# Query, key, value and forget-logit projection by one level of Strassen's algorithm

## The chip, the cores and the metric

The kernel runs on one NeuronCore of a Trainium2 chip: TensorE (PE in the profile; its weight loads are shown apart as PEld), VectorE (DVE), ScalarE (ACT), GpSimd (POOL) and SyncE (SP, which here only issues DMAs). The metric is the device time of one execution in microseconds; the profiled execution is a single run of its own.

## The reference, cut to what matters

One layer of an encoder over 2048 tokens of width 1024: a mixing block (attention with forget gates in eight heads of 64, beside a multi-scale pooling branch), cross-attention to 256 memory tokens, and a gated feed-forward part. All in float32. The change touches only the first projection and what is made of it:

```python
xn = rmsnorm(h, g_mix[l])
z = jnp.einsum('bsd,dc->bsc', xn, w_in[l])      # 1024 -> 2056 columns
q = z[..., :512]; k = z[..., 512:1024]; v = z[..., 1024:1536]
p_in = z[..., 1536:2048]                        # pooling branch
f_logit = z[..., 2048:] + b_forget[l]           # 8 columns
q = rmsnorm(head_split(q, 8, 64), g_q_fox[l])
k = rmsnorm(head_split(k, 8, 64), g_k_fox[l])
```

Queries, keys, values and forget logits are 1544 of the columns; the 512 of the pooling branch are projected by other code.

## The kernel before

Products are made to nearly float32 accuracy: `split` cuts an operand into a rounded part `hi` (ScalarE copies it to type fp32r) and the rest `lo` (VectorE subtracts, `sub_hi`, line 55, or with a gain `split_gain`, lines 173 and 174), and `mm3` (lines 60 to 62) issues three matmuls, hi·hi, hi·lo and lo·hi, into one PSUM bank.

The stages in order: (1) the keys and values of the memory tokens (`kv`, 96 matmuls 512 wide), while the weights `w_qkvf` (1024 by 1544) are loaded and split; (2) the projection studied here; (3) the pooling branch, in eight blocks of 256 tokens; (4) attention, cross-attention and feed-forward, which the change doesn't touch.

In stage 2 the weights lie split in SBUF, eight slices of 128 rows by 1544 columns. A loop runs over eight blocks `b` of 256 tokens and two tiles `i` of 128 tokens in each. For a tile, `project` makes four PSUM banks of 386 columns, each over eight slices of the 1024 rows: 4·8·3 = 96 matmuls. The transposed input `xT` is loaded once, in tiles of 128 by 2 by 256 (`x_load`), and split (`x_split`), which also makes the squares for the token norm; `token_sums` adds them up over partitions by matmuls against ones (line 199), two tiles at a time, and `token_rstd` makes the reciprocal root on GpSimd. ScalarE moves the banks to SBUF times that factor (`scaled`, line 324). `normed_heads` splits the values and makes the head norms, `split_heads` scales queries and keys by norm and by gain (lines 355, 357) and splits them, and `to_heads` turns them by four groups of four TensorE transposes (line 369, into a PSUM tile that ScalarE copies, line 371) and stores them to DRAM (`qkT`). Values go to `vd`.

In this stage all five engines run in the written order (`tc.manual_schedule`): what is written ahead of an instruction on its engine also goes ahead on the chip. The stage ends with the pooling projection of block 0 (`project_p`); behind it only TensorE's order is fixed, and the other engines' is made by the framework's scheduler.

The lines that carry the stage:

```python
for k, n in ([(k, n) for k in range(KD) for n in ns] if k_outer else [(k, n) for n in ns for k in range(KD)]):
    sl = slice(n * ZB, (n + 1) * ZB)
    mm3(zps[n][:], (hs[k][:, ts], ls[k][:, ts]), (whi[k][:, sl], wlo[k][:, sl]), k == 0, k == KD - 1)
```

Of the kernel before, what the change touches and what calls it, by code (L numbers as in the profile page):

```python
# [33 lines left out]
QKVF = 3 * FOXW + H  # L34
ZB = QKVF // 4

# [4 lines left out]
def block_kernel(ctx: ExitStack, tc: tile.TileContext, x, xT, memT, cols, rows, w_qkvf, w_p, w_pool, w_out,  # L41
# [52 lines left out]
    gqs = cst.tile([P, 2, DH], F32, name="gqs")  # L94

    dve.tensor_scalar(out=gqs[:, 0, :], in0=gqf, scalar1=-(DH ** -0.5), scalar2=None, op0=ALU.mult)
    dve.tensor_copy(gqs[:, 1, :], gkf)
    gqm = cst.tile([P, 1], F32, name="gqm")
    dve.tensor_scalar(out=gqm[:], in0=gq_mem, scalar1=P ** -0.5, scalar2=None, op0=ALU.mult)
    rstd = cst.tile([P, NT], F32, name="rstd")  # L100
# [24 lines left out]
    class Slots:  # L125

        def __init__(self, pl, shape, name, n):
            self.pl, self.shape, self.name = pl, shape, name
            self.free = list(range(n))

        def take(self, dt):
            n = self.free.pop(0)
            return n, self.pl.tile(self.shape, dt, tag=f"{self.name}{n}", name=f"{self.name}{n}", bufs=1)

    xsl = Slots(xp, [P, 2, B], "xl", 9)
    xlow = []

    def x_load(b, src=xTk, qs=range(4)):

        while len(xlow) > 4:  # L140
            xsl.free.append(xlow.pop(0))
        tiles = []
        for q in qs:
            n, raw = xsl.take(F32)
            sp.dma_start(raw[:], src[:, 2 * q:2 * q + 2, b * B:(b + 1) * B])
            tiles.append((n, raw))
        return tiles

    def x_split(tiles, part=None, qs=range(4)):

        for q in qs:
            n, raw = tiles[q]
            hi = xp.tile([P, 2, B], F32R, tag="xhi", name="xhi", bufs=8)
            act.copy(hi[:], raw[:])
            if part is not None:
                sq = xp.tile([P, 2, B], F32, tag="xsq", name="xsq", bufs=2)[:] if q else part
                act.activation(sq, raw[:], AF.Square, scale=1.0 / 32.0)
                if q:
                    pool.tensor_tensor(out=part, in0=part, in1=sq, op=ALU.add)
            m, lo = xsl.take(F32R)  # L160
            sub_hi(lo[:], raw[:], hi[:])
            xsl.free.append(n)
            xlow.append(m)
            tiles[q] = hi, lo
# [18 lines left out]
    whi = [None] * KD  # L183
    wlo = [None] * KD
    wph = [None] * KD
    wpl = [None] * KD
    HIS = 16

    with ExitStack() as c0:
        was = ExitStack()  # L190
        wa = opened(was, "wa", side="right")
        tpp = opened(xstack, "tpp", space=PSUM)

        def token_sums(part):

            ssp = tpp.tile([P, 2], F32, tag="ss", name="ss", bufs=1)
            for j in range(2):
                for c in range(2):
                    pe.matmul(ssp[:, j:j + 1], lhsT=part[:, c, j * P:(j + 1) * P], rhs=ones[:, 0:1], start=c == 0,
                              stop=c == 1)  # L200
            return ssp

        def token_rstd(ssp, outp):
            ms = xp.tile([P, 2], F32, tag="ms", name="ms", bufs=2)
            dve.tensor_copy(ms[:], ssp[:])
            rsqrt(outp, ms[:])


        kvs = ExitStack()
        kvp = opened(kvs, "kvp", space=PSUM)  # L210
        first = in_order(EN.DVE, EN.Activation, EN.Pool, EN.SP)
        first.__enter__()
        kv = [[kvp.tile([P, MW], F32, name=f"kv{m}{a}") for a in range(2)] for m in range(2)]
        wk = [None] * KD
        wsl = Slots(wa, [P, QKVF], "wl", KD)
        w_raw = [None] * KD

        def w_in_hi(k, dt):

            return wa.tile([P, QKVF], dt, tag=f"wh{k}", name=f"wh{k}", bufs=1)  # L220

        def load_kv(k):
            wk[k] = w_in_hi(k, F32)[:, :2 * MW]
# [8 lines left out]
        def load_w_in(k):  # L232

            n, raw = wsl.take(F32) if k < KD - 1 else (None, slab(3))
            w_raw[k] = n, raw[:, :QKVF]
            sp.dma_start(w_raw[k][1], w_qkvf[k * P:(k + 1) * P, :])

        def split_w_in(k):
            n, raw = w_raw[k]
            whi[k] = w_in_hi(k, F32R)  # L240
            wlo[k] = wsl.take(F32R)[1]
            split(whi[k][:], wlo[k][:], raw, g_mix[:, k:k + 1])
            wsl.free.append(n)
# [5 lines left out]
        xt = x_load(0)  # L249
        mpart = xp.tile([P, 2, B], F32, tag="part", name="part", bufs=1)  # L250
        mr = cst.tile([P, 2], F32, name="mr")
        for k in range(KD):
# [4 lines left out]
            if k == 3:  # L257
                token_rstd(token_sums(mpart), mr[:])
            for m in range(2):
                ms_ = slice(m * P, (m + 1) * P)  # L260
                for a in range(2):
                    as_ = slice(a * MW, (a + 1) * MW)
                    mm3(kv[m][a][:], (mh[:, ms_], ml[:, ms_]), (wh[:, as_], wl[:, as_]), k == 0, k == KD - 1)
            if k < 4:
                load_kv(k + 4)
            if k == 1:
                load_w_in(0)
            if k == 3:
                for c in range(1, KD):
                    load_w_in(c)  # L270
            if k == 6:
                split_w_in(0)
            if k == 5:
                part = xp.tile([P, 2, B], F32, tag="part", name="part", bufs=1)
                x_split(xt, part[:])
        split_w_in(1)
        mks_ = [slab(n, dt=F32R)[:].rearrange("p (a c) -> p a c", a=2) for n in (2, 0)]
        mkv = [t_[:, a] for t_ in mks_ for a in range(2)]
        mkh, mkl = (t_.rearrange("p (h m) -> p h m", h=MH) for t_ in mkv[:2])
        mvh, mvl = (t_.rearrange("p (m c) -> p m c", m=2) for t_ in mkv[2:])  # L280
        mks, msk = ([zp.tile([P, MH, P], F32, tag="st", name="mks", bufs=4) for _ in range(2)] for _ in range(2))
        for m in range(2):
            act.activation(mks[m][:].rearrange("p h d -> p (h d)"), kv[m][0][:], AF.Copy, scale=mr[:, m:m + 1])
            split_gain(mvh[:, m], mvl[:, m], kv[m][1][:], mr[:, m:m + 1])
        for n in range(2, 4):
            sp.dma_start(mkvd[n], f(mkv[n]))
        kvs.close()

        def mem_key_norms():
            for m in range(2):  # L290
                act.activation(msk[m][:], mks[m][:], AF.Square)
                ms = zp.tile([P, MH], F32, tag="mkms", name="mkms", bufs=2)
                dve.tensor_reduce(out=ms[:], in_=msk[m][:], axis=AX.X, op=ALU.add)
                rk = zp.tile([P, MH], F32, tag="mkr", name="mkr", bufs=2)
                rsqrt(rk[:], ms[:], 1.0 / P)
                dve.tensor_tensor(out=mks[m][:], in0=mks[m][:], in1=rk[:].unsqueeze(2).to_broadcast([P, MH, P]),
                                  op=ALU.mult)

        def mem_keys():
            for m in range(2):  # L300
                tp = tpp.tile([P, MH, P], F32, tag="tp", name="tp", bufs=3)
                for h in range(MH):
                    pe.transpose(tp[:, h], mks[m][:, h], ident[:])
                ms_ = slice(m * P, (m + 1) * P)
                split_gain(mkh[:, :, ms_], mkl[:, :, ms_], tp[:], gk_mem)
            for n in range(2):
                sp.dma_start(mkvd[n], f(mkv[n]))


        with ExitStack() as c1:  # L310
            zpp = opened(xstack, "zpp", space=PSUM)

            def project(i, j, hs, ls, ns, k_outer=False):
                zps = {n: zpp.tile([P, ZB], F32, tag="z", name="zps", bufs=4) for n in ns}
                ts = slice(j * P, (j + 1) * P)
                for k, n in ([(k, n) for k in range(KD) for n in ns] if k_outer else [(k, n) for n in ns for k in range(KD)]):
                    sl = slice(n * ZB, (n + 1) * ZB)
                    mm3(zps[n][:], (hs[k][:, ts], ls[k][:, ts]), (whi[k][:, sl], wlo[k][:, sl]), k == 0, k == KD - 1)
                return zps

            def scaled(i, zps):
                z = slab(i % 2)
                for n in zps:
                    act.activation(z[:, n * ZB:(n + 1) * ZB], zps[n][:], AF.Copy, scale=rstd[:, i:i + 1])
                return z

            ssp = token_sums(part)
            for k in range(2, KD):
                split_w_in(k)
            token_rstd(ssp, rstd[:, 0:2])  # L330
            mem_key_norms()
            zps0 = project(0, 0, *x_parts(xt), range(4), True)
            def normed_heads(i, z):

                vq = slab(3)
                vr = vq[:, :1024].bitcast(F32R).rearrange("p (h a d) -> p h a d", h=H, a=2)
                zv = z[:, 1024:1536].rearrange("p (h d) -> p h d", h=H)
                act.copy(vr[:, :, 0, :], zv)
                sub_hi(vr[:, :, 1, :], zv, vr[:, :, 0, :])
                sp.dma_start(vd[:, :, i, :].rearrange("h p c -> p h c"), vq[:, :1024].rearrange("p (h c) -> p h c", h=H))  # L340
                dve.tensor_tensor(out=fl[:, :, i], in0=z[:, 1536:1544], in1=bfor, op=ALU.add)

                qn = vq[:, 1024:]
                qf = qn.rearrange("p (h d) -> p h d", d=DH)
# [1162 lines left out]
```

## Time and profile before

| what | us |
|---|---|
| median of three runs | 2573.42 (2572.7 to 2578.22) |
| the profiled execution | 2576.41 |
| its span, first to last instruction | 2574.7 |
| memory keys and values, matmuls | from 8.3 to 36.2 |
| the projection's 1536 matmuls | from 37.0 to 335.7 |
| end of that to the loop of the pooling branch in its third block | 335.7 to 385.6 |

A row of the timeline gives the start in us, the duration in us, the engine, the line of the source, the operation, output and inputs, shape and how many were merged, and in brackets the idle time ahead of it and what ended it. A row of windows gives, for each engine, busy us and the number of instructions, then the granted clock of TensorE, the busy share of the DMA engines and GB/s. Durations of matmuls overlap, since one starts while the one before is still draining: what a matmul costs is the distance between starts. The same holds, by about a tenth of a microsecond, for the other engines.

### The profile page before, as it was taken

What the parts mean: (1) busy time and instruction counts of PE and PEld (TensorE: products, weight loads), DVE (VectorE), ACT (ScalarE), POOL (GpSimd) and SP (SyncE); (2) the same over time, 40 slices, a digit from 0 to 9 for tenths busy, and PEclk for the clock granted to TensorE, in tenths of its full rate; (3) what the DMA queues carried; (4) which work ended last, traced back from release to release, by engine and by line L of the source; (5) the groups of instructions that cost most, each with busy time, mean ns of one, the idle gap of its engine ahead of it and who ended that gap; (6) DMA issues with size and microseconds to landing.
All of it is one profiled execution on the core that took longest, in us unless ns stands there. A gap on an engine that the chain in (4) does not pass through costs nothing.

```text
span 2574.7 us, 36909 instructions
## 1 busy us (share of the span) xinstructions
PE 2535.0 (98%) x13133; PEld 2179.9 (85%) x13133; DVE 1700.4 (66%) x2933; ACT 1248.2 (48%) x2375; POOL 818.3 (32%) x1087
## 2 busy tenths in 40 slices
PE   8999999999999989999999999999999999999999
PEld 7999989978888878888778888888888888888887
DVE  6444376569999965554777787756766666665554
ACT  6454442158888865444543433334543333333443
POOL 3343240025455443333525445430001222222000
PEclk9999999999999999999999999999999999999999
DMA  6443365346445132222464555447773332334766
GB/s 244 127 127 111 119 217 173 125 137 166 124 113 159 59 127 86 83 82 87 160 221 177 181 180 193 147 159 268 245 261 130 103 122 103 118 108 168 235 207 205
DMA packets 204777, 396.20 MB, mean 154 GB/s; under 512 B 24368, under 2 KB 99888, under 8 KB 193840
## 3 DMA queue, kind: packets, MB, share of 16 engines
q1 hardware_dynamic: 175088, 296.30, 35.9%
q0 software_dynamic: 29504, 97.54, 9.8%
q8 instruction: 103, 1.69, 0.3%
q14 instruction: 82, 0.67, 0.1%
HBM read 268.85 MB, written 124.91 MB: 153 GB/s over the span
## 4 chain that ended last, share of the span: by engine, by line
PE 41%; issue 8%; DVE 1%; POOL 1%; ACT 0%; DMA 0%; POOLq 0%; SPq 0%; DVEq 0%; ACTq 0%
PE bk L62 13%; PE bk L60 13%; PE bk L61 13%; DVE ww L55 0%; POOL out_dram L1400 0%; PE mmps L60 0%; DMA xraw<-hTd 0%; PE mmps L61 0%; PE mmps L62 0%; DVE t L971 0%; PE bk L939 0%; DVE cb L55 0%; ACT ww L178 0%; ACT pm L1073 0%; ACT s3h L178 0%
## 5 line engine op out<-in xcount | busy, mean ns | idle before, releaser
L55 DVE TENSOR_TENSOR ww<-draw,ww 128x512 fp32r<-128x512 f32 x308 | 205.0, 704 | 156.6 <-ACT ww L178 156.4
L178 ACT CAST ww<-draw 128x512 fp32r<-128x512 f32 x308 | 179.4, 620 | 220.1 <-PE bk L62 171.1
L55 DVE TENSOR_TENSOR ww<-graw,ww 128x512 fp32r<-128x512 f32 x220 | 178.4, 817 | 110.2 <-ACT ww L178 109.8
L61 PE MATMUL bk<-ww,ww 128*128 128x512 f32 x616 | 239.8, 389 | 0.0
L60 PE MATMUL bk<-ww,ww 128*128 128x512 f32 x616 | 239.6, 389 | 0.0
L62 PE MATMUL bk<-ww,ww 128*128 128x512 f32 x616 | 239.6, 389 | 0.0
L178 ACT CAST ww<-graw 128x512 fp32r<-128x512 f32 x220 | 136.0, 622 | 181.0 <-PE bk L62 160.9
L55 DVE TENSOR_TENSOR pl<-tp,ph 128x512 fp32r<-128x512 f32 (+3 forms) x296 | 176.9, 599 | 26.2 <-ACT ph L783 24.4
L702 ACT ACTIVATE s<-s,mx 128x1024 f32<-128x1024 f32 (+2 forms) x192 | 173.7, 905 | 4.5 <-DVE mx L696 2.6
L767 PE MATMUL tp<-ident,s 128*128 128x128 f32 x1088 | 171.0, 273 | 4.9 <-DVE pl L55 4.3
L60 PE MATMUL zps<-wh,xhi 128*128 128x386 f32 x512 | 175.7, 343 | 0.1
L61 PE MATMUL zps<-wl,xhi 128*128 128x386 f32 x512 | 173.6, 339 | 0.0
L62 PE MATMUL zps<-wh,xl 128*128 128x386 f32 x512 | 173.2, 338 | 0.0
L783 ACT CAST ph<-tp 128x512 fp32r<-128x512 f32 (+3 forms) x296 | 148.8, 514 | 33.6 <-PE tp L767 28.5
L767 PEld LDWEIGHTS tp<-ident,s 128*128 128x128 f32 x1088 | 132.8, 140 | 32.9 <-DVE pl L55 8.1
L1400 POOL DMA_DIRECT2D out_dram<-o x32 | 17.3, 540 | 382.9 <-DVE o L1397 377.2
L62 PE MATMUL bk<-qs,ww 128*128 128x512 f32 x352 | 137.2, 390 | 1.1 <-DVE ww L55 1.1
L60 PE MATMUL bk<-qs,ww 128*128 128x512 f32 x352 | 137.9, 392 | 0.3 <-ACT s L1319 0.3
L61 PE MATMUL bk<-kh,ww 128*128 128x512 f32 x352 | 137.0, 389 | 0.0
L60 PE MATMUL bk<-kl,ww 128*128 128x512 f32 x352 | 136.9, 389 | 0.0
L61 PE MATMUL bk<-cb,ww 128*128 128x512 f32 x352 | 136.9, 389 | 0.0
L62 PE MATMUL bk<-kl,ww 128*128 128x512 f32 x352 | 136.9, 389 | 0.0
(549 smaller groups left out, 7254.8 us busy)
## 6 DMA issues: line engine op xcount, KB each, us to landing
graw<-in_w_gu_dram SPq DMA_DIRECT2D x44, 1024.0 KB, 5.4
draw<-in_w_down_dram SPq DMA_DIRECT2D x66, 256.0 KB, 4.3
xl<-in_xT_dram SPq DMA_DIRECT2D x64, 256.0 KB, 4.8
qkT<-st SPq DMA_DIRECT2D x64, 256.0 KB, 2.7
wdr<-in_w_down_dram SPq DMA_DIRECT2D x22, 512.0 KB, 4.3
vd<-cb SPq DMA_DIRECT2D x16, 512.0 KB, 3.3
xr<-in_x_dram SPq DMA_DIRECT2D x16, 512.0 KB, 3.4
qs<-qkT SPq DMA_DIRECT2D x8, 1024.0 KB, 6.8
```

What stands on the lines that cost most here:

```text
L55: (eng or dve).tensor_tensor(out=lo, in0=src, in1=f(hi), op=ALU.subtract)
L60: pe.matmul(ps, lhsT=sh, rhs=mh, start=first, stop=False, skip_group_check=goes_on)
L61: pe.matmul(ps, lhsT=sh, rhs=ml, start=False, stop=False, skip_group_check=goes_on)
L62: pe.matmul(ps, lhsT=sl, rhs=mh, start=False, stop=last, skip_group_check=goes_on)
L178: act.copy(hi, raw)
L702: act.activation(s[:, sl], s[:, sl], AF.Exp, bias=ng, scale=-1.0, accum_out=l[:, q, g:g + 1])
L767: pe.transpose(tp[:, q * P:(q + 1) * P], unit["rows"][q][:, j * P:(j + 1) * P], ident[:])
L783: act.copy(ph[:, sl], tp[:, sl])
L1400: pool.dma_start(out[rows_, cs], o)
```

## The change

The 1024 rows are cut into two halves and the columns, too, and tokens are taken in pairs of tiles of 128. A block product of 2 by 2 blocks is then made with seven products in place of eight, in Winograd's form of Strassen's algorithm. The columns are done in two groups, each with half of the queries, keys, values and (in the second) the forget logits: group 0 is 2 by 384 columns, group 1 is 2 by 388. A unit is one pair of tiles in one group: 16 units, the first eight over group 0, the last eight over group 1 in the reverse order of tokens.

Of the weights of a group, `Weights` makes seven operands, each 4 slices wide and split into hi and lo: `b11`, `b21`, `b22` as they are, `t1` to `t4` from sums. Of a pair of tokens, `Tokens` makes seven: `x11`, `x12`, `x22`, and `s1` to `s4`. A product is 4·3 = 12 matmuls (`product_z`), in two halves of six; so a unit has 84 matmuls, 16 units 1344. Two of a unit's products (`x22·t4` and `s4·b22`) are made during the unit behind it. PSUM sums what it can; the rest is summed in SBUF: four banks are copied (`fresh`) and three added (`more`).

What else moves: the gain `g_mix` is multiplied into the weights beforehand, on GpSimd (ScalarE for one block); the token norm comes from rows of `x`, loaded apart (32 DMAs) and squared on ScalarE with an accumulating output, and `token_sums` goes but for the memory tokens; the gains of queries and keys are multiplied into the keys alone, on GpSimd; the values are scaled and split on GpSimd; `xT` is read twice (once for each group, but for one pair), by tiles with rows of 512 bytes. The weights of group 1 are loaded, gained, summed and split while group 0 runs; they go into the same places as those of group 0, so each can be made only after the last use of the old one. The pooling projection of block 0 lies between the last unit's late products. The order of every job is a number, in steps of half a product (14 in a unit).

```diff
-            def project(i, j, hs, ls, ns, k_outer=False):
-                zps = {n: zpp.tile([P, ZB], F32, tag="z", name="zps", bufs=4) for n in ns}
...
+GROUPS = [[[(a * 256, 256), (1024 + a * 128, 128)] for a in range(2)],
+          [[(512 + a * 256, 256), (1280 + a * 128, 128), (1536 + a * 4, 4)] for a in range(2)]]
...
+            def gain(self, kh, a, eng=pool, h=None):
...
+            SUMS = dict(t1=("e", (0, 1), (0, 0)), t3=((0, 1), (1, 1), (0, 1)), t2=((0, 0), (1, 1), "e"),
+                        t4=((1, 0), (1, 0), (0, 0)))
+            def sums(self, nm, eng, h=None):
...
+                eng.tensor_tensor(out=o, in0=p_, in1=q_, op=ALU.subtract)
...
+            def fresh(self, t, a, ps):
+                if t and a and not self.g:
+                    dve.tensor_copy(self.out(t, a), ps[:, :self.w])
+                else:
+                    act.copy(self.out(t, a), ps[:, :self.w])
+            def more(self, t, a, ps):
+                o = self.out(t, a)
+                dve.tensor_tensor(out=o, in0=ps[:, :self.w], in1=o, op=ALU.add)
...
+            def gain(self, t):
+                hd = self.heads(t)
+                pool.tensor_tensor(out=hd, in0=hd, in1=gqk[:].unsqueeze(1).unsqueeze(1)
+                                   .to_broadcast([P, 2, 4, DH]), op=ALU.mult)
+            def value_scale(self, t):
+                zv = self.z[:, t, :, 256:384]
+                pool.tensor_tensor(out=zv, in0=zv, in1=self.rs(t).unsqueeze(1).to_broadcast([P, 2, 128]), op=ALU.mult)
...
+        def product_z(ps, tk, xn, wt, wn, first_, half):
+            hi, lo = tk.ops[xn][:2]
+            wh, wl = wt.ops[wn]
+            for k in range(2 * half, 2 * half + 2):
+                mm3(ps[:, :wt.w], (hi[:, k], lo[:, k]), (wh[:, k], wl[:, k]), first_ and k == 0, k == 3, not first_)
...
+            pos = {"s1": ("x22", "x21", "x22", ALU.add, dve), "s3": ("x21", "x11", "x21", ALU.subtract, pool),
+                   "s2": ("x11", "x22", "x11", ALU.subtract, dve), "s4": ("x12", "x12", "x11", ALU.subtract, pool)}
...
+        for nm, st, lst, eng in (("b11", 2, (3, 6), pool), ("b21", 6, (8,), dve), ("t2", 11, (15,), dve), ("t1", 14, (16, 18), pool),
+                                 ("t3", 17, (19,), dve), ("t4", 22, (24, 26), pool), ("b22", 24, (26,), dve)):
+            at(L, st, w1.hi, nm)
...
+        def step_z(u, st):
+            n, half = divmod(st, 2)
+            if u == 0 and n in (4, 5):
+                n = 9 - n
+            xn, wn = (("x11", "b11"), ("x22", "t4"), ("x12", "b21"), ("s4", "b22"), ("s2", "t2"), ("s1", "t1"), ("s3", "t3"))[n]
+            v = u - 1 if n in (1, 3) else u
+            if v >= 0 and v < 2 * NU:
+                a, b, c = sets[v]
+                product_z((a, a, c, b, a, b, a)[n], toks[v], xn, wts[v // NU], wn, n in (0, 2, 5), half)
...
+        for u in range(2 * NU):
+            begin(u)
+            for st in range(14):
+                step_z(u, st)
+                for job in first_plan.pop(st, ()):
+                    job()
+                jobs(u, st)
```

In the order that the build gives each engine, attention and everything behind it stand as before.

More of the change, by code (lines that the diff above doesn't have):

```diff
@@ L276, in block_kernel @@
[L276 to L289, printed above, removed]
+                    mm3(kv[m][a], (mh[:, ms_], ml[:, ms_]), (wh[:, as_], wl[:, as_]), k == 0, k == KD - 1)
+            if k == 4:
+                w0.gain(0, 1)
+            if k == 5:
+                w0.put("b11")
+                w0.gain(1, 0)
+            if k == 6:
+                tok.put("x11")
+                w0.sums("t1", pool)
+            if k == 7:
+                w0.put("b21")
+                tok.put("x12")
+                tok.put("x22")
+                w0.gain(1, 1, act)
+                w0.hi("t1")
+                tok.sum("x22", "x21", "x22", ALU.add, dve)
+                tok.sum("x21", "x11", "x21", ALU.subtract, pool)
@@ new lines, in block_kernel @@
+        soon(0, w0.hi, "t2")
+        soon(0, w0.lo, "t2", dve)
+        soon(0, tok.hi, "s2")
+        soon(0, tok.lo, "s2")
+        soon(0, tok.hi, "s3")
+        soon(0, tok.lo, "s3")
+        soon(1, evict, 0, 1)
+        soon(1, tok.sum, "x12", "x12", "x11", ALU.subtract, pool)
+        soon(1, tok.done, "x11")
+        soon(1, w0.hi, "t3")
+        soon(1, w0.lo, "t3", dve)
+        soon(6, w0.sums, "t4", pool)
+        soon(11, evict, 0, 5)
+        soon(11, evict, 0, 6)
+        soon(11, evict, 0, 3)
```

725 lines of the change are left out of this document (490 added, 235 removed), and 20 rows, old and new, of the table ORDER.

## The prediction

> **What bounds the kernel now.** I read the page first, for the busy shares and the slices, then windows cut at the stage's edges, then TensorE's timeline for what one matmul costs, and last the timelines of the other engines, for what the change gives them.
>
> ```profile
> span 2574.7 us, 36909 instructions
> PE 2535.0 (98%) x13133; PEld 2179.9 (85%) x13133; DVE 1700.4 (66%) x2933; ACT 1248.2 (48%) x2375; POOL 818.3 (32%) x1087
> 37.00:335.70 298.70, 298.56 (x1826) 297.17 (x1826) 139.48 (x151) 145.09 (x241) 103.75 (x74) 1.00 0.39 119
> 335.70:385.60 49.90, 44.15 (x341) 42.62 (x340) 37.65 (x67) 26.16 (x46) 22.28 (x25) 0.93 0.82 252
> ```
>
> The stage is the row 37.0 to 335.7: 298.7 us in which TensorE has no idle time at full clock, while DVE, ACT and POOL are busy 47%, 49% and 35%. So matmuls taken out shorten it, until another engine is the slower one. What is one matmul worth? Not its duration; the distance between starts:
>
> ```profile
> 115.22 0.46 PE L369 MATMUL tp<-identr,kl 128*128 128x128 f32 x4
> 115.51 1.02 PE L199 MATMUL ss<-ones,part 128*128 128x1 f32 x8
> 116.40 0.43 PE L60 MATMUL zps<-wh,xhi 128*128 128x386 f32 x1
> 116.66 0.34 PE L61 MATMUL zps<-wl,xhi 128*128 128x386 f32 x1
> ...
> 129.01 0.34 PE L62 MATMUL zps<-wh,xl 128*128 128x386 f32 x1
> 129.19 1.13 PE L369 MATMUL tp<-identr,kl 128*128 128x128 f32 x12
> 130.15 0.41 PE L60 MATMUL zps<-wh,xhi 128*128 128x386 f32 x1
> 130.40 0.34 PE L61 MATMUL zps<-wl,xhi 128*128 128x386 f32 x1
> ```
>
> The second to the 72nd of these matmuls start 12.35 us apart over 70 steps: 0.1764 us each, half of the 0.34 that a row shows. Four transposes take 0.29 us (115.22 to 115.51), the token sums 0.89 (to 116.40). Each break costs 0.07 more, as the first matmul behind it holds the next for 0.25.
>
> **What TensorE saves.** Seven products for eight: 16 units of 84 matmuls are 1344, against 16 tiles of 96, 1536. 192 · 0.1764 = 33.9 us. Widths of 384 and 388 for 386 change nothing on average. The token sums go, eight times 0.89: 7.1 us. The 256 transposes stay, but in 64 groups of four where there were 16 groups of twelve and 16 of four: 32 breaks more, +2.2 us. Sum: **-38.8 us**. A unit is then 84 · 0.1764 + 4 · 0.36 = 16.3 us, 16 of them 260 us. That is what the other engines must keep up with.
>
> **What the other engines get in a unit.** Durations, again by distance of starts:
>
> ```profile
> 112.70 0.69 DVE L55 TENSOR_TENSOR cb<-kh,cb 128x512 fp32r<-128x512 f32 x1 [5.11 <-ACT cb L338]
> 113.31 0.17 DVE L341 TENSOR_TENSOR fl<-kh,rowt 128x8 f32<-128x8 f32 x1
> 113.66 1.22 DVE L347 TENSOR_REDUCE zms<-cb 128x16 f32<-128x1024 f32 x1 [0.18 <-ACT cb L345]
> 358.21 0.42 DVE L509 SCALAR_TENSOR_TENSOR mixed<-s,pT 128x256 f32<-128x256 f32 x1
> 358.55 0.71 DVE L507 TENSOR_TENSOR s<-s 128x530 f32<-128x530 f32 x1
> 124.80 1.53 ACT L324 ACTIVATE qs<-zps,rstd 128x386 f32<-128x386 f32 x3 [2.47 <-POOL rstd L71]
> 129.87 1.55 ACT L371 COPY st<-tp 128x512 f32<-128x512 f32 x3
> 113.42 0.36 SPq L340 DMA_DIRECT2D vd<-cb  x1
> 133.14 0.55 SPq L388 DMA_DIRECT2D wpr<-in_w_p_dram  x1
> L780 POOL TENSOR_TENSOR ph<-pf,ones 128x512 fp32r<-128x512 f32 x24 | 25.4, 1056 | 2.6 <-ACT pf L779 2.2
> L71 POOL TENSOR_TENSOR zrq<-zms,mhalf 128x16 f32<-128x16 f32 x16 | 50.3, 3145 | 1.3
> L71 POOL TENSOR_TENSOR rstd<-ms,mhalf 128x2 f32<-128x2 f32 x8 | 5.7, 714 | 0.7
> ```
>
> - ACT: a copy of 512 columns costs 0.52, of 386 some 0.5. Seven `hi` of tokens 3.6, three `fresh` 1.5, four `turned` 2.1, squares and head splits 2.8, and in group 0 four squares of token rows at about 0.7: 12.8 us of 16.3, and 10.5 in group 1. It fits.
> - DVE: 0.61 for 512 columns with two SBUF inputs, 0.34 for 256. Seven `lo`, two token sums and two head splits: 11 · 0.61 = 6.7; four `scale` 1.4; three `more` and one copy from PSUM, estimated at 0.47 from the 0.61 scaled by width, 1.9; two norm sums 1.2. Together 11.2 us. It fits if it is left alone.
> - POOL: 1.06 for 512 columns, so about 0.6 for 256 and 1.6 for the 776 of half a weight block. Two token sums 2.1, values scaled and split 2.4, two roots of eight columns (estimated 2.4 with their additions, between the 0.71 of two columns and the 3.15 of sixteen) 4.8, group norm 1.3: 10.6 us; in group 1 the key gain, 2.1, stands for the norm: 11.4.
> - SP: 14 DMAs a unit at the 0.36 to 0.55 us of its rows, at most 8 us. Bytes: x, its rows and the outputs are 3.5 MB a unit in group 0 (2.5 in group 1). By the window (119 GB/s at a share of 0.39) that is 11.5 us of 16.3; with a quarter of the next weights, 0.8 MB, 14.1. Hidden, with little to spare.
>
> Each fits alone, but DVE and POOL don't work beside each other freely:
>
> ```profile
> 100.65 5.76 POOL L159 TENSOR_TENSOR part<-part,xsq 128x512 f32<-128x512 f32 x3
> 100.71 2.32 DVE L355 TENSOR_TENSOR cb<-qs,zrq 128x1024 f32<-128x1024 f32 x1 [1.10 <-POOL zrq L71]
> 103.06 2.19 DVE L357 TENSOR_TENSOR cb<-cb,gqs 128x1024 f32<-128x1024 f32 x1
> ...
> 118.71 1.23 DVE L355 TENSOR_TENSOR cb<-kh,zrq 128x1024 f32<-128x1024 f32 x1 [3.16 <-POOL zrq L71]
> ```
>
> DVE's line 355 takes 1.23 us alone and 2.32 beside POOL; POOL's three additions take 5.76, and 3 · 1.06 + 2 · 1.23 = 5.6: their times add up, as if one waited for the other each time. The Trainium skill says so ("SBUF — State Buffer", Who interferes with whom): the pair of ports that the two share is an exclusive lock, held for a whole instruction, and a DVE instruction with two SBUF inputs takes it against a GpSimd one that reads SBUF. The trace agrees, with the 5.76. In a unit DVE holds two-input work for 8.1 us and POOL for 4.5 (6.6 in group 1; the roots, mostly arithmetic, left out): 12.6 to 14.7 of 16.3, tight but under it. I take 0.4 us of TensorE wait for each of 13 ordinary units, **+5** (bounds 0 and 2 us a unit, 26).
>
> **The change of groups.** Around units 7 and 8 group 1's operands are made in the places of group 0's: over some 26 half products, 30 us, POOL gets ten half blocks, 16 us, and DVE five blocks of 1536 at about 1.7, 8.3. Unit 8 uses unit 7's tokens, which saves 5.5 us on DVE and 2.1 on POOL. Two-input work is then 8.1 · 1.86 + 8.3 - 5.5 = 17.9 on DVE and 4.5 · 1.86 + 16 - 2.1 = 22.3 on POOL: 40 us in 30. Some of it can slip, since `t4` and `b22` are used a unit later; I take **+6** (0 to 16).
>
> **The start.** The first unit's operands hang together, and no products cover them.
>
> ```profile
> 22.47 1.61 POOL L71 TENSOR_TENSOR mr<-ms,mhalf 128x2 f32<-128x2 f32 x1
> 26.96 1.58 ACT L173 ACTIVATE wh<-wl,colt 128x1544 fp32r<-128x1544 f32 x1
> 30.44 1.82 DVE L174 SCALAR_TENSOR_TENSOR wl<-wl,colt,wh 128x1544 fp32r<-128x1544 f32 x1
> 35.94 0.40 PE L62 MATMUL kv<-kh,xl 128*128 128x512 f32 x1
> ```
>
> POOL can begin the gains behind `mr`, at 24; three of them and the first sum are four blocks of 1536 at 3.2, about 4 with DVE beside them: done at 36 and 40. TensorE ends the memory products at 36, as before, has `x11·b11` (operands ready about 30) to 38, then waits for `b21` (gain 36, `hi` 1.6, `lo` 1.7: 39.5), then for `t1` (sum 40, `hi` 42, `lo` behind another sum on DVE, 44.5), and for `t3`. Waits of 1.5, 3 and about 1 us, and then `t4` and `b22` for unit 1: I take **+8** (3 to 15).
>
> **The end.** The last unit's late products, block 0 of the pooling projection and the last transposes stand among each other. Before, TensorE was idle 5.8 us in the 49.9 behind the stage; the chain of the last unit is 25 to 28 half products long after its own. I take 0 (-3 to +8).
>
> **Sum.** -38.8 + 5 + 6 + 8 + 0 = -19.8. The profiled execution took 2576.4 (span 2574.7 and 1.7 around it), so 2556.6; the median of the runs is 3.0 lower, so about **2554**. Own range 2543 to 2565. Less than 0.2% (5 us) can't be told from no change.
>
> **Rivals.**
> - *Everything is covered.* TensorE never waits but for the shortest start, +3: 2573.4 - 35.8 = 2538. For it: all engines are under 80% alone. Against: the pair of DVE and POOL.
> - *DVE and POOL become one engine, and it is the bound.* If nothing of one hides beside the other, the stage is DVE 16 · 11.1 = 178 and, for the new weights (8.3) and the pooling projection's (7 · 0.61), 13; and POOL 16 · 4.5 + 8 · 2.1 = 89 and 32 for weights (20 half blocks): 312 us against 260. Then -38.8 + 52 + 8 = +21: 2594, slower. It decides from a unit of (298.7 - 8) / 16 = 18.2 us on. For it: the additive rows; against: DVE's 3 us from PSUM and sums, POOL's 5 us of roots, and idle time can lie beside each other. [...]
> - *Late operands.* Start +15, change of groups +16, end +8: 2573.4 - 38.8 + 39 = 2574, no change. The windows show a lower granted clock (0.93) where TensorE has gaps, which would make each wait dearer.
> - *Loads.* x is read twice by shorter rows; if they move at half the rate of the window, units 1 to 6 need some 25 us for 16.3, which adds 52: 2606, slower. Against: most of the stage's bytes already move in rows of 512.
>
> **Chances.** My forecast 0.45, all covered 0.18, DVE and POOL as one 0.18, late operands 0.15 (of which 0.08 within 0.2%, 0.07 slower), loads 0.04. Faster 0.63, same 0.08, slower 0.29. The range goes from the covered case with the shorter end, 2533, to the joint engine, 2594.
>
> **What would show it.** Right: 1344 matmuls 0.176 apart, units of 16.3 to 17 us, waits of TensorE on DVE `lo` rows at 38 to 60 us and around 165 to 200. Wrong: `lo` rows of 1 us and more in every unit and units over 18 us (the lock), TensorE waits that end at DMAs (loads), or a long idle time behind the last unit.

## The result

The changed kernel takes 2610.94 us (median of four runs, 2609.92 to 2613.23) against 2573.38 for the kernel before on the same chip: a ratio of 1.0143, 95% interval 1.0126 to 1.0161. It is slower by 37.6 us; the prediction said 2554, in a range up to 2594. The profiled execution has a span of 2608.2 us.

The page of the changed kernel, its first lines:

```profile
span 2608.2 us, 37292 instructions
PE 2512.3 (96%) x12877; PEld 2146.1 (82%) x12877; DVE 1846.9 (71%) x3136; ACT 1300.2 (50%) x2530; POOL 986.9 (38%) x1239
```

TensorE is busy 23 us less, DVE and POOL 147 and 169 us more. The whole loss lies ahead of the loop of the pooling branch: its first matmul (`oo`) starts at 420.1, where it was 385.8. The next view is TensorE's timeline of the changed kernel; the first matmul of `x11·b11` marks the start of a unit (5 and 6 are shown), the last row the end of the stretch:

```profile
147.29 0.34 PE L63 MATMUL zps<-b11h,x11h 128*128 128x384 f32 x1
...
163.73 0.34 PE L63 MATMUL zps<-b11h,x11h 128*128 128x384 f32 x1
...
420.08 0.48 PE L63 MATMUL oo<-wop00h,poh 128*128 128x512 f32 x1
```

Unit 5 takes 16.4 us, the 16.3 that the prediction worked out for a unit in which nothing waits. The others don't. From the same marks, in us (unit 0 has 10.6 of work, as two of its products are made later):

| stretch | length | above 16.3 a unit |
|---|---|---|
| memory products end at 42.4, before at 36.2 | | 6.2 |
| unit 0 | 21.1 | 10.5 |
| unit 1 | 17.7 | 1.4 |
| units 2, 3, 4 | 23.9, 21.8, 20.4 | 17.2 |
| units 5, 6 | 16.4, 17.0 | 0.8 |
| units 7, 8 (change of groups) | 22.9, 25.2 | 15.5 |
| units 9 to 14 (group 1) | 18.8, 18.8, 18.6, 18.2, 18.8, 19.0 | 14.5 |
| unit 15 to `oo` | 79.0 | 7.0 |

The last entry is what is left of the whole: 34.3 lost and 38.8 not needed make 73.1, less the others. The last column holds waits of TensorE and, behind some of them, matmuls at a lower clock. Busy time in two stretches, in windows of the changed kernel (engines as in the table of before, then granted clock, DMA share, GB/s):

```profile
180.00:229.00 49.00, 37.52 (x207) 35.53 (x205) 39.88 (x44) 32.60 (x58) 46.53 (x36) 0.93 0.40 114
229.00:341.00 112.00, 99.96 (x600) 96.42 (x599) 102.45 (x137) 65.15 (x133) 84.14 (x72) 1.00 0.56 157
```

The first row is the change of groups: POOL is busy 95% of it. In units 9 to 14 (the second) DVE is busy 91% and POOL 75%, at a DMA share of 0.56; TensorE, which had no idle time in this stage before, is at 89%. What it waited for, the largest of the waits of TensorE between 37 and 341 us (total, number, longest); the same view of the kernel before is empty:

```profile
PE tp L568 <- DVE kl L58: 11.7, 6, 2.9
PE tp L568 <- DVE cb L58: 7.5, 7, 2.9
PE zps L63 <- ACT qs L495: 6.5, 4, 3.0
PE zps L64 <- DVE t1l L58: 4.5, 1, 4.5
```

Most ends at DVE. Why DVE is late is seen in its rows beside POOL's. First the start (timelines of DVE, POOL and TensorE of the changed kernel):

```profile
30.43 3.76 DVE L181 SCALAR_TENSOR_TENSOR qs<-t1h,colt,qs 128x1024 fp32r<-128x1024 f32 x1
34.12 4.01 DVE L58 TENSOR_TENSOR x11l<-xr,x11h 128x512 fp32r<-128x512 f32 x1
...
28.86 4.25 POOL L262 TENSOR_TENSOR r(1, 0)_222<-r(1, 0)_222,colt 128x1536 f32<-128x1536 f32 x1
33.08 4.51 POOL L272 TENSOR_TENSOR re<-r(0, 1)_219,r(0, 0)_212 128x1536 f32<-128x1536 f32 x1
...
34.25 0.80 PE L64 MATMUL kv<-qs,xlh 128*128 128x512 f32 x1 [4.95 <-DVE qs L181]
34.84 0.63 PE L65 MATMUL kv<-qs,xll 128*128 128x512 f32 x1
35.27 0.63 PE L63 MATMUL kv<-qs,xlh 128*128 128x512 f32 x1
...
40.32 0.40 PE L63 MATMUL kv<-kh,xlh 128*128 128x512 f32 x1
40.56 0.40 PE L64 MATMUL kv<-kh,xlh 128*128 128x512 f32 x1
```

A subtraction of 512 columns, 0.61 us in the prediction's rows, takes 4.01 while POOL makes a sum of weights: it ends half a microsecond behind POOL's. The low part of the memory weights ahead of it is held up by POOL's gain in the same way, TensorE waits 4.95 us for it, and behind that wait its matmuls start 0.43 us apart for more than 5 us, and 0.24 apart later. That is why the memory products, which the change doesn't touch, end 6.2 us later.

And a unit of group 1, in small (timelines of DVE and POOL, from 285 us on):

```profile
285.45 1.48 DVE L331 TENSOR_TENSOR xr<-xr 128x512 f32<-128x512 f32 x1
...
289.06 1.90 DVE L530 SCALAR_TENSOR_TENSOR qs<-qs,rstd,zrq 128x256 f32<-128x256 f32 x2 [1.06 <-POOL zrq L74]
...
285.08 1.30 POOL L511 TENSOR_TENSOR qs<-qs,gqk 128x512 f32<-128x512 f32 x1 [1.70 <-ACT cb L543]
...
288.99 1.29 POOL L331 TENSOR_TENSOR xr<-xr 128x512 f32<-128x512 f32 x1
```

Each DVE row that falls on a POOL row is longer by about what is left of POOL's.

### The profile page after: what moved, and what is told of

Read it like the earlier page. It is cut to its first block, busy times and chain, and to the rows that moved or that the text cites. A ratio compares the mean times of both kernels' runs of the same rounds, so it can differ in the third digit from the quotient of the medians.

```text
span 2608.2 us, 37292 instructions
## 1 busy us (share of the span) xinstructions
PE 2512.3 (96%) x12877; PEld 2146.1 (82%) x12877; DVE 1846.9 (71%) x3136; ACT 1300.2 (50%) x2530; POOL 986.9 (38%) x1239
## 4 chain that ended last, share of the span: by engine, by line
PE 70%; issue 9%; DVE 2%; ACT 2%; POOL 1%; DMA 1%; POOLq 0%; SPq 0%; DVEq 0%; ACTq 0%
PE bk L65 13%; PE bk L63 13%; PE bk L64 13%; PE acc L1188 5%; PE sps L1125 5%; PE tp L1203 4%; PE mmps L63 3%; PE mmps L65 3%; PE mmps L64 3%; PE tp L1312 1%; PE oo L65 1%; PE oo L64 1%; PE oo L63 1%; PE zp L63 1%; PE zp L64 1%
## 5 line engine op out<-in xcount | busy, mean ns | idle before, releaser
L1836 POOL DMA_DIRECT2D out_dram<-o x32 | 17.3, 542 | 382.6 <-DVE o L1833 376.9
L64 PEld LDWEIGHTS bk<-ww,ww 128*128 128x128 f32 x616 | 115.6, 188 | 24.3
L63 PEld LDWEIGHTS bk<-ww,ww 128*128 128x128 f32 x616 | 115.6, 188 | 24.2
L65 PEld LDWEIGHTS bk<-ww,ww 128*128 128x128 f32 x616 | 115.6, 188 | 23.7
```

Source lines behind the costliest of these rows:

```text
L63: pe.matmul(ps, lhsT=sh, rhs=mh, start=first, stop=False, skip_group_check=goes_on)
L64: pe.matmul(ps, lhsT=sh, rhs=ml, start=False, stop=False, skip_group_check=goes_on)
L65: pe.matmul(ps, lhsT=sl, rhs=mh, start=False, stop=last, skip_group_check=goes_on)
L1836: pool.dma_start(out[rows_, cs], o)
```

## The experiments

**The theory and its rival.** Theory: DVE instructions with two SBUF inputs stand still while POOL reads SBUF, so what the change gives to POOL costs DVE as much time as POOL takes, and everything queued on DVE behind it; POOL's work is then dearer than the same work done on DVE itself. Rival: DVE is simply full (91%) or the operands are made too late, and then giving DVE more work makes the kernel slower. Three experiments move POOL's two-input work away, a part each, to VectorE or ScalarE; the fourth has all three. Each starts from the changed kernel.

The start: the gains of group 0's weights that POOL made go to ScalarE, the sums to VectorE.

```diff
-                w0.gain(0, 0)
-                w0.gain(0, 1)
-                w0.gain(1, 0)
-                w0.sums("t1", pool)
+                w0.gain(0, 0, act)
+                w0.gain(0, 1, act)
+                w0.gain(1, 0, act)
+                w0.sums("t1", dve)
...
-        soon(0, w0.sums, "t3", pool)
+        soon(0, w0.sums, "t3", dve)
-        soon(6, w0.sums, "t4", pool)
+        soon(6, w0.sums, "t4", dve)
```

(The first `s3` and `s4` likewise. The gains and `t1` also stand later in the order.)

> Only the start differs from the changed kernel (2611 us): the gains of group 0's weights go from GpSimd to ScalarE, its sums t1, t3, t4 and the first token sums s3, s4 from GpSimd to VectorE. Theory A, the shared ports: VectorE's subtractions of 4 to 5 us there (0.7 to 1.7 alone) wait for GpSimd blocks, so without these the memory products end near 36 us instead of 42.4 and unit 1 begins near 50 instead of 63.5: about 2598. Theory B, the order of the jobs and the length of VectorE's own queue: VectorE gets three blocks of 1.7 and three of 0.6 more, 7 us in front of the same operands: 2611 to 2618.

Measured 2603.91 us (one run). Unit 0 starts at 35.5 (42.4) and takes 16.8 us (21.1): 11.2 us of the start's 16.7 are gone. 2.9 of them are lost again in units 1 to 14, most in units 1, 4 and 9 (18.9, 22.0 and 20.0).

The units' own work: token sums, key gain and the values' low part to VectorE, the values' scaling to ScalarE.

```diff
-"s3": ("x21", "x11", "x21", ALU.subtract, pool)
+"s3": ("x21", "x11", "x21", ALU.subtract, dve)
-"s4": ("x12", "x12", "x11", ALU.subtract, pool)
+"s4": ("x12", "x12", "x11", ALU.subtract, dve)
...
-                pool.tensor_tensor(out=hd, in0=hd, in1=gqk...
+                dve.tensor_tensor(out=hd, in0=hd, in1=gqk...
...
-                pool.tensor_tensor(out=zv, in0=zv, in1=self.rs(t)...
+                act.activation(zv, zv, AF.Copy, scale=self.rs(t))
...
-                sub_hi(vr[:, :, :, 1], zv, vr[:, :, :, 0], pool)
+                sub_hi(vr[:, :, :, 1], zv, vr[:, :, :, 0])
```

> Only the units' own jobs differ: token sums s3 and s4, the low part of the values and the gain of the keys go from GpSimd to VectorE, the scaling of the values to ScalarE; GpSimd keeps the roots and the weights. Theory A: VectorE's 17 us in a unit of group 1 are some 11.5 of work and 6 of waiting at the ports; it gets 3.1 us of work more and loses most of the 6, so units 9 to 15 come down from 18.7 to about 16.8 us and units 2 to 6 by about 1: about 2592. Theory B: VectorE is long as it is and becomes longer: units of 20 us, about 2630.

Measured 2592.26 us (one run). Units 10 to 14 take 16.2 to 17.2 us (18.2 to 19.0).

The weights of group 1: gains, sums and low parts to VectorE.

```diff
-            at(*g_[h], w1.gain, kh, a, pool, h)
+            at(*g_[h], w1.gain, kh, a, dve, h)
...
-            at(6, (6, 9.2)[h], w1.sums, "t1", pool, h)
+            at(6, (6, 9.2)[h], w1.sums, "t1", dve, h)
...
-("b11", 2, (3, 6), pool)
+("b11", 2, (3, 6), dve)
```

(`t3` and `t4`, sums and low parts, likewise.)

> Only the weights of group 1 differ: their gains, sums and low parts are made on VectorE instead of GpSimd. Theory A: units 2 to 4 and 7 to 8, 19 us above 16.3 a unit each on average together some 33 us, lose about 12 of it: about 2599. Theory B: VectorE gets some 25 us more in seven units that are already long: about 2620.

Measured 2602.26 us (one run). Units 7 and 8 take 19.5 and 20.7 us (22.9 and 25.2).

All three together:

> The three edits together; GpSimd keeps only the roots, the norms and the memory tokens' sums. Theory A: the gains add up, -13 -19 -12: about 2567, near the kernel before. Theory B: 2640 or more, with VectorE busy throughout and TensorE waiting for it in every unit.

Measured 2573.94 us (2570.52 to 2575.76); to the kernel before 1.0001 (0.9992 to 1.0011). The parts gained 7.0, 18.7 and 8.7 us, 34.4 in all; together they gain 37.0, the whole of what the change had lost. They lie 6, 0, 3 and 7 us above theory A's times, and 7, 38, 18 and 66 us below the lowest of theory B's. VectorE, already the busiest engine beside TensorE, became faster with more work. Its rows in group 1, timeline of the kernel with all three:

```profile
251.99 1.42 DVE L335 TENSOR_TENSOR xr<-xr 128x512 f32<-128x512 f32 x2
253.32 0.88 DVE L533 SCALAR_TENSOR_TENSOR qs<-qs,rstd,zrq 128x256 f32<-128x256 f32 x2
```

The pair of scalings takes 0.88 us (1.90), a token sum 0.67 (1.48). Moving work does two things, though: it empties POOL, and it changes who makes what when. The next two separate them, from the kernel with all three moved: POOL gets work back that nobody waits for. In the first it adds 128 columns of a tile of its own, 8 times a unit in group 0 and 12 times in group 1; in the second, two fills of 176 columns stand for each addition, which read nothing from SBUF.

```diff
+    junk = xp.tile([P, 176], F32, name="junk")
+    def idle_add(n):
+        for _ in range(n // 256):
+            pool.tensor_tensor(out=junk[:, :128], in0=junk[:, 48:], in1=ones[:], op=ALU.add)
```

```diff
-            pool.tensor_tensor(out=junk[:, :128], in0=junk[:, 48:], in1=ones[:], op=ALU.add)
+            pool.memset(junk[:], 0.0)
+            pool.memset(junk[:], 0.0)
```

> The kernel of e4 (2574 us), and GpSimd adds 128 columns of a tile of its own, which nobody waits for, once or twice at each of the places that were its own before: 8 additions a unit of group 0, 12 of group 1, about 5 us of a unit in which it has roots of 5 us and is else idle. Theory A, the shared ports: VectorE waits for each, and the time goes up by 10 to 25 us. Theory B, VectorE was only relieved of waiting for GpSimd's results: within 3 us of 2574.

> As e7, but in place of each addition GpSimd sets a tile of 176 columns to zero twice, which reads no SBUF. If the ports are held only against reading, as the Trainium skill has it (SBUF — State Buffer, SBUF: two separate sides), the time stays within 3 us of e4's 2574; if any GpSimd instruction stops VectorE, it goes up as in e7.

Measured 2589.72 us and 2574.17 us (one run each): 15.8 more, and 0.2. The groups of DVE and POOL between 229 and 330 us, for the additions:

```profile
L342 DVE TENSOR_TENSOR xr<-xr 128x512 f32<-128x512 f32 x21 | 16.6, 793 | 0.2
L542 DVE SCALAR_TENSOR_TENSOR kh<-kh,rstd,zrq 128x256 f32<-128x256 f32 x12 | 7.6, 669 | 0.9 <-POOL zrq L74 0.9
L532 DVE TENSOR_REDUCE zms<-sq 128x8 f32<-128x512 f32 x10 | 6.8, 676 | 0.0
L131 POOL TENSOR_TENSOR junk<-junk,ones 128x128 f32<-128x128 f32 x66 | 42.4, 642 | 4.3
```

and for the fills:

```profile
L343 DVE TENSOR_TENSOR xr<-xr 128x512 f32<-128x512 f32 x20 | 13.7, 685 | 0.2
L543 DVE SCALAR_TENSOR_TENSOR kh<-kh,rstd,zrq 128x256 f32<-128x256 f32 x12 | 5.3, 480 | 3.8 <-POOL zrq L74 3.8
L533 DVE TENSOR_REDUCE zms<-sq 128x8 f32<-128x512 f32 x12 | 8.1, 678 | 0.0
L131 POOL MEMSET junk<- 128x176 f32 x68 | 16.7, 246 | 3.2
```

Two fills take 0.49 us for the 0.64 of an addition. Beside additions the token sum takes 793 ns for 685 and the scaling 669 for 480; the reduction, with one input, keeps its 0.68. Beside fills all keep the times that they have with neither (687, 479 and 680 ns). Nor does DVE wait longer for POOL's results: for the roots it waits 0.9 us with the additions and 3.8 with the fills. So POOL holds DVE up where it reads SBUF, and not by being busy. The rule of the Trainium skill ("SBUF — State Buffer", SBUF: two separate sides) says the same of two-input DVE instructions against GpSimd ones that read SBUF, with the lock held for the whole instruction. The trace agrees for additions, subtractions and gains, by the 4.01 us above, and by the fills and the reduction here; POOL's roots are an exception (last section).

**What is left of the loss.** With all three moves TensorE still waited once for long, in the last stretch (its timeline):

```profile
368.09 0.75 PE L571 MATMUL tp<-identr,cb 128*128 128x128 f32 x4 [10.94 <-ACT st L576]
```

This is a transpose of the last unit, written ahead of pooling work that was ready. The next kernel puts it behind one more piece of that work:

```diff
-                        if n == 1:
+                        if n == 2:
                             last_turn(1)
```

> The kernel of e4 (2574 us), and the last four transposes of the projection stand one block of the pooling branch later. In e4 TensorE waits 10.9 us for them, behind a ScalarE copy that the scheduler put late, at a granted clock of 0.67. Theory: that wait is TensorE's alone, so all of it comes out, with the slow matmuls behind it: 2560 to 2563. Rival: the copy is late because ScalarE and VectorE are late at that place, and the wait moves to the next product of the pooling branch: 2570 or more.

Measured 2570.19 us (2568.65 to 2573.78); to the kernel before 0.9987 (0.9977 to 0.9996). That is the rival's time, and in the rival's way: 6 of the 11 us came back at the next matmul in the order, whose operand is late, too:

```profile
362.15 0.58 PE L63 MATMUL op<-mxh,wpoolh 128*128 128x256 f32 x1 [5.98 <-ACT mxh L954]
```

This kernel is a hair faster than the one before, and none of those that follow and compute everything is faster beyond the spread of the runs. Its units 2 and 4 still take 22.3 and 20.8 us, and TensorE's waits between 37 and 306 us are now these (its view of waits, the two longest rows):

```profile
PE zps L63 <- ACT qs L498: 6.6, 5, 2.8
PE tp L571 <- DVE kl L58: 5.1, 4, 1.7
```

The waits on the keys' low parts are less than half of what they were (11.7), those on ScalarE's copies the same (6.5). Its windows there:

```profile
100.00:140.00 40.00, 35.81 (x225) 34.85 (x223) 32.16 (x61) 29.48 (x67) 16.72 (x16) 1.00 0.92 265
140.00:180.00 40.00, 38.36 (x235) 37.13 (x234) 37.30 (x64) 32.52 (x69) 20.29 (x15) 1.00 0.65 192
```

The DMA engines are at 0.92 in the first, DVE at 93% in the second. The rest of the experiments start from it and ask why. The row loads of the tokens, moved from SyncE's queue to ScalarE's:

```diff
-                sp.dma_start(rows_[:], x[i * P:(i + 1) * P, a * 512:(a + 1) * 512])
+                act.dma_start(rows_[:], x[i * P:(i + 1) * P, a * 512:(a + 1) * 512])
```

> The kernel of e5, and the token rows for the norms are fetched by ScalarE's own DMA queue instead of SyncE's. In e4 SyncE waits 17.9 us of units 1 to 4 for ScalarE to have read the rows before, with the loads of the next tokens queued behind it, and units 2 and 4 take 22.5 and 23.5 us. Theory: those units come to 18 or 19 us, 6 to 10 us less than e5, about 2553. Rival: the DMA engines, busy 0.85 of the time there, are the limit and not the queue: within 2 us of e5.

Measured 2574.03 us (2572.38 to 2577.77), units 2 and 4 at 24.7 and 24.6: neither the theory nor the rival. Between 50 and 130 us SyncE's queue had waited 17.3 us until ScalarE had read the rows before, and it no longer does, and the units became longer: taking the rows off it was no cure, though ScalarE's queue may have its own delay. Then two kernels with less to load in these units:

```diff
-                sp.dma_start(rows_[:], x[i * P:(i + 1) * P, a * 512:(a + 1) * 512])
+                sp.dma_start(rows_[:, :16], x[i * P:(i + 1) * P, a * 512:a * 512 + 16])
```

> The kernel of the tail's experiment (2570.2 us), with 16 of the 512 columns of each half row of tokens loaded and the squares taken of a tile of ones, so it leaves out the true norm of the tokens; ScalarE's work stays and some 8 MB of loads go. Theory A: the units 2 to 5 are long (22.3 and 20.8 us, DMA share 0.92) because the loads of the rows, of the token parts and of group 1's weights share the DMA engines; then units 2 and 4 come down to 17 to 18 us and the time to 2558 to 2564 us. Rival B: they are long because of the order in which the turns of the heads are written, and the units and the time stay (2567 to 2573 us).

```diff
-        for (kh, a), ld_, g_ in (((0, 0), (1, 6), ((2, 3.2), (2, 9.2))), ((1, 0), (2, 6), ((3, 3.2), (3, 9.2))),
-                                 ((0, 1), (3, 13), ((4, 9.2), (5, 3.2))), ((1, 1), (4, 13), ((5, 9.2), (6, 3.2)))):
+        for (kh, a), ld_, g_ in (((0, 0), (4, 6), ((5, 9.2), (5, 12.2))), ((0, 1), (4, 13), ((6, 0.2), (6, 3.2))),
+                                 ((1, 0), (5, 6), ((6, 4.2), (6, 8.2))), ((1, 1), (5, 13), ((6, 10.2), (6, 13.2)))):
```

> The kernel of the tail's experiment (2570.2 us), with the four loads of group 1's weights moved from units 1 to 4 into units 4 and 5, and their gains into units 5 and 6: nothing is left out. Theory A (the DMA engines are the limit of units 2 to 5): units 2 and 4 fall to 17 to 19 us, later units gain at most 2 us each, the time is 2560 to 2567 us. Rival B (not the DMA engines): units 2 and 4 stay at 20 us and more, the time is 2568 to 2576 us, more by what the later gains add ahead of the change of groups.

Measured 2565.84 us (2564.7 to 2566.48) without the rows, units 2 and 4 at 20.5 and 19.6; and 2570.00 us (2568.04 to 2571.99) with the weights later, units 2 and 4 at 22.4 and 18.0, but unit 7 at 20.5 for 17.6. The first lies between its two theories. The second has the rival's time and, in unit 4, the theory's length; unit 7 takes back what unit 4 gave. The largest waits of TensorE in units 2 and 4 move with the row loads: they are 2.05 and 2.75 us in the kernel with the tail's change, 3.97 and 3.85 with the rows on ScalarE's queue, and without the rows the first is gone and the second 1.50.

Then DVE. One kernel takes the scaling of the sums of squares off POOL, to shorten the chain that leads to the keys' low parts; the other takes work off DVE.

```diff
+                dve.tensor_scalar(out=self.ms[t][:], in0=self.ms[t][:], scalar1=1.0 / DH, scalar2=EPS, op0=ALU.mult, op1=ALU.add)
...
-                rsqrt(rq[:], self.ms[t][:], 1.0 / DH)
+                pool.tensor_tensor(out=rq[:], in0=self.ms[t][:], in1=mhalf[:, :H], op=ALU.pow)
```

> The kernel of the tail's experiment (2570.2 us), with the scaling of the sums of squares of 8 heads (128x8, 1.3 us on POOL behind a busy DVE, 24 times in 220 us) done by VectorE right behind its reduction; POOL is left the root alone. Nothing is left out. Theory A (the exclusive ports also hold POOL up: its short instructions wait for DVE, and the chain from the norms to the keys' low parts, on which TensorE waits 1.2 to 1.9 us in the units of group 0, is longer by that): the chain shortens by 1 us and more, the waits on the low parts shrink, the time is 2560 to 2566 us. Rival B (DVE's 97% of busy time sets the units, not the chain): the time is 2568 to 2573 us.

```diff
-                eng.tensor_tensor(out=self.r[o][1][:], in0=self.r[p_][1][:], in1=self.r[q_][1][:], op=op)
+                c_ = lambda n: self.r[n][1][:, :, :8]
+                eng.tensor_tensor(out=c_(o), in0=c_(p_), in1=c_(q_), op=op)
...
-                    dve.scalar_tensor_tensor(out=hd[:, a], in0=hd[:, a], scalar=self.rs(t),
+                    dve.scalar_tensor_tensor(out=hd[:, a, :, :8], in0=hd[:, a, :, :8], scalar=self.rs(t),
```

> The kernel of the tail's experiment (2570.2 us) with less work on VectorE: the token sums and the scaling of the heads are taken on 8 columns of each 128 or 64 alone, so the rest of both is left out; the number of instructions, the loads and all other work stay. That is some 4 times 0.6 and 4 times 0.3 us, 3.6 us of VectorE a unit in group 0 and 1.2 to 3.6 in group 1. Theory A (VectorE, 97% busy once it does POOL's share, now sets the length of the long units): units 2, 4 and 8 fall from 22.3, 20.8 and 21.2 us to 17 to 18.5, the others to 16.3 to 17, and the time to 2548 to 2556 us. Rival B (loads and written order set them): units 2 and 4 stay above 20 us and the time at 2563 to 2571 us.

The first: 2571.15 us (2569.68 to 2572.05), no gain, as the rival had it. The instruction on POOL that went had taken 1.27 us; the root behind it became longer, 1.97 us for 1.78. POOL's groups between 60 and 280 us, with the tail's change alone:

```profile
L74 POOL TENSOR_TENSOR zrq<-zms,mhalf 128x8 f32<-128x8 f32 x24 | 42.6, 1776 | 2.0
L70 POOL TENSOR_SCALAR zms<-zms 128x8 f32<-128x8 f32 x24 | 30.4, 1267 | 108.6 <-DVE zms L523 108.6
```

The second splits the question in two: 2556.84 us (2556.13 to 2559.40). In group 1 units 9 to 14 fall from 16.5 to 17.5 us to 16.2 or 16.3, and TensorE has no idle time left (windows in these units, with the tail's change alone and with less on DVE):

```profile
213.00:295.00 82.00, 80.53 (x484) 77.90 (x483) 72.06 (x140) 56.91 (x116) 28.82 (x20) 1.00 0.62 176
213.00:295.00 82.00, 82.00 (x506) 81.44 (x506) 61.78 (x147) 61.02 (x123) 21.07 (x21) 1.00 0.63 183
```

There DVE's own work was the limit, at 88% busy before and 75% now; whether by its sum or by the chain that runs through it isn't told apart. But units 2 and 4 stay, at 20.5 and 22.0 us. The wait in unit 4 is there in both, 2.75 and 3.10 us; in the kernel with the tail's change, timelines of ScalarE and TensorE:

```profile
120.65 0.63 ACT L358 ACTIVATE rows<-rows 128x512 f32<-128x512 f32 x1 [1.74 <-DMA rows<-in_x_dram]
123.80 0.62 ACT L320 CAST x12h<-xr 128x512 fp32r<-128x512 f32 x1 [1.75 <-DMA xr<-in_xT_dram]
...
124.85 0.44 PE L63 MATMUL zps<-t2h,s2h 128*128 128x384 f32 x1 [2.75 <-ACT qs L498]
```

ScalarE stands 1.7 us at a square whose rows and 1.7 us at a `hi` whose tokens haven't landed; queued behind them is the copy of a product out of its PSUM bank, and TensorE waits 2.75 us for that bank. So here a load does end TensorE's wait, through an engine that works in the written order. Units 2 to 4 still lose 12.7 us with the tail's change, and 9.7 without the rows. How that divides between loads and the order of the jobs stays open: the runs differ by 1 to 3 us in these units without an edit there (unit 4 took 23.5 us in one kernel and 20.8 in the next), and turning the heads later, which would test the order, wasn't tried.

## Why the prediction was wrong

- **What TensorE saves, -38.8: right.** Unit 5 took 16.4 us in the changed kernel, and six units 16.2 to 16.3 where DVE had less to do, against 16.3 predicted.
- **Steady units, +5: wrong, and the step that failed.** They lost 33.9 us (1.4, 17.2, 0.8 and 14.5), past the bound of 26. For group 1 the prediction had the rule and the additive rows, added up the two-input work of both engines, 12.6 to 14.7 us of 16.3, and called that "tight but under it". But DVE runs its instructions in order, and all of its 11.1 us must pass, not only the 8.1 with two inputs; POOL's 6.6 come on top wherever they meet one of those. 11.1 + 6.6 = 17.7 is the sum that should have been made for group 1, DVE was busy 17.1 us a unit in the window of units 9 to 14 (102.45 over six), and 18.2 to 19.0 is what they took, over 18, as the prediction's sign for the lock had it. (Leaving out POOL's roots was right, see the last section.) This was the rival *DVE and POOL become one engine*, with 0.18: right in cause, with its units at or over the 18.2 us at which nothing is gained, and with 2594 still 17 us short.
- **In group 0 most of the cause is another one.** Units 2 to 4 lost 17.2 us in the changed kernel and 15.6 without POOL's work (12.7 in the kernel with the tail's change): most of this is not the ports. The prediction counted 14.1 us of loads in 16.3 as hidden "with little to spare"; it left out that a load that is late by 2 us stops ScalarE, and ScalarE TensorE. That is shown for part of the loss; the rest stays open.
- **The start, +8: 16.7.** The waits were put at `b21`, `t1` and `t3`. The largest came earlier: POOL's gains held DVE up under the memory products (6.2 us), at a point that the prediction took as unchanged ("ends the memory products at 36, as before"). With this work off POOL, unit 0 began at 35.5.
- **The change of groups, +6: 15.5**, its upper bound. The 40 us of two-input work in 30 were worked out, and then taken to slip. Off POOL, units 7 and 8 lose 5.3.
- **The end, 0: 7.0**, inside the bound of 8. A transpose of the last unit stood in front of ready work:

```profile
403.41 0.75 PE L568 MATMUL tp<-identr,cb 128*128 128x128 f32 x4 [7.28 <-ACT st L573]
```

- *Everything is covered*, 2538, never came near. *Late operands* had the start, the change of groups and the end nearly right (15, 16 and 8 against 16.7, 15.5 and 7.0), but as a case of its own: it came together with the lock, in part from the same cause. The chances were given as if the rivals excluded one another, and the range ended at the dearest single one. (Its low end, by its own terms, is 2535: 2538 less 3.)

So the change did what it says, 192 matmuls less at their price, and paid with about 73 us of waits and of slow matmuls behind them. Half of that, 37 us, went when POOL's two-input work did; of the rest some is DVE's own work, some loads, and some isn't told apart.

## What to carry to other kernels

Before work is given to an idle POOL, add its time with SBUF inputs (but for the roots) to the whole busy time of DVE in the same stretch, not to DVE's two-input part, and compare that with the stretch: here 17.7 us against 16.3 was already too much. If the sum doesn't fit, do the work on DVE, which takes 0.61 us for the 1.06 of POOL, or on ScalarE; POOL's fills cost 0.2 us here, less than runs differ by. And an engine that works in the written order hands each late operand to everything behind it: a copy that frees a PSUM bank should do better ahead of a cast whose load may be late, though no run here tried that order.

## What the runs showed of the hardware

- The length of a DVE instruction hardly matters when it meets POOL. In the last stretch of the changed kernel, sixteen columns took 1.27 us beside a subtraction of POOL's, and 0.16 later (timelines of DVE and POOL):

```profile
391.46 1.53 POOL L58 TENSOR_TENSOR wop00l<-wr,wop00h 128x512 fp32r<-128x512 f32 x1 [9.96 <-ACT wop00h L185]
...
391.75 1.27 DVE L946 TENSOR_TENSOR mixed<-mixed,pT 128x16 f32<-128x16 f32 x1
...
398.78 0.16 DVE L946 TENSOR_TENSOR mixed<-mixed,pT 128x16 f32<-128x16 f32 x1
```

- It works the other way, too. In the kernel with the tail's change POOL's scaling of eight columns takes 0.20 us beside a DVE instruction that reads a PSUM bank, and 4.93 behind a run of DVE instructions with two SBUF inputs; it ends 0.05 us behind the last of them, `kl` (timelines of POOL and DVE):

```profile
193.97 0.20 POOL L70 TENSOR_SCALAR zms<-zms 128x8 f32<-128x8 f32 x1 [5.88 <-DVE zms L523]
...
200.34 4.93 POOL L70 TENSOR_SCALAR zms<-zms 128x8 f32<-128x8 f32 x1 [4.46 <-DVE zms L523]
...
204.54 0.68 DVE L58 TENSOR_TENSOR kl<-kh,kl 128x512 fp32r<-128x512 f32 x1
```

- POOL's roots don't hold DVE up, though they read SBUF, too: with all three moves, DVE's subtractions of 512 columns that lie wholly inside a root take 0.685 us (18 of them), and 0.685 with POOL idle.
- A wait of TensorE costs more than its length. After the 4.95 us its matmuls were 0.43 apart for more than 5 us, for 0.24 later. Far shorter waits were enough: 2.40 us in unit 2 of the changed kernel (then 0.32 apart for nearly 5 us), 2.89 in its unit 8 (0.32 for over 2 us), and, with the tail's change, 1.88 in unit 8:

```profile
200.47 0.44 PE L63 MATMUL zps<-t3h,s3h 128*128 128x388 f32 x1 [1.88 <-ACT qs L498]
...
202.01 0.53 PE L64 MATMUL zps<-t3l,s3h 128*128 128x388 f32 x1
202.34 0.53 PE L65 MATMUL zps<-t3h,s3l 128*128 128x388 f32 x1
```

The starts are 0.33 apart for some 3 us. In the same kernel a wait of 2.98 us at the start left the distance at 0.18:

```profile
42.27 0.45 PE L64 MATMUL zps<-t1l,s1h 128*128 128x384 f32 x1 [2.98 <-DVE t1l L58]
...
43.33 0.34 PE L64 MATMUL zps<-t1l,s1h 128*128 128x384 f32 x1
43.51 0.35 PE L65 MATMUL zps<-t1h,s1l 128*128 128x384 f32 x1
```

The Trainium skill ("TensorE: Matmul & The Clock Gate", Part 1) puts the fall to half rate behind an idle window of about 3.4 us. Here it came after 1.88 us and once not after 2.98, so the measured waits decide: from some 2 us on it has to be reckoned with, and the length of the wait alone doesn't tell.
